# The gate stage of a hybrid decoder block: convolution copies begun by POOL, sums and merges spread over later pieces, sigmoids left in PSUM, gate groups in another order

## The chip, the cores and the metric

The kernel runs on one core of a Trainium2 chip. The metric is the device time of one execution in microseconds. The kernel before was run three times: 1552.89, 1555.58 and 1556.43 us, a median of 1555.58 us. A fourth execution, taken with the profiler, lasted 1552.18 us.

## The reference

One decoder layer over 256 tokens of width 2048, in float32. A normalised input goes through one wide projection `w_in`. Its columns feed two mixers: a chunked gated linear attention with four heads (q, k, v, the decay), and a short gated convolution. Both are merged under sigmoid gates, projected by `w_out`, and followed by a gated feed-forward layer and a last norm. The part that the change touches is this (cut):

```python
def causal_depthwise_conv(u, w):
    s = u.shape[1]
    up = jnp.pad(u, ((0, 0), (CONV_K - 1, 0), (0, 0)))
    return sum(up[:, j:j + s, :] * w[j] for j in range(CONV_K))
...
    y_a = (o * jax.nn.silu(g_out.reshape(b_, s, GLA_HEADS, GLA_HEAD_V))).reshape(b_, s, GLA_VALUE_DIM)
    y_b = gate_b * causal_depthwise_conv(gate_c * xc, conv_w)
    merged = jax.nn.sigmoid(merge_a) * y_a + jax.nn.sigmoid(merge_b) * y_b
    return jnp.einsum('bse,ed->bsd', merged, w_out)
```

## The kernel before

**Pieces.** All weights stream through the core in pieces of 128 x 1024 floats. For each piece SP loads `raw` from DRAM (line 274, or 211 for the sums below), ACT casts it to a rounded part `hi` (line 217), DVE subtracts to get the rest `lo` (line 222), and PE multiplies in three passes, `hi` by the low part of the activations, `lo` by the high part, `hi` by the high part (lines 326 to 328). There are five `raw`, six `hi` and five `lo` buffers. `take` keeps the loading `LOOK = 5` pieces ahead of the piece that PE uses; so the instructions for a later piece stand early in the rows of ACT and DVE, and how far DVE really is ahead of PE at a moment is called its **lead** here.

**Ticks.** Each used piece advances a counter, the tick. `later(n, fn)` and `at(tick, fn)` put other work into the program at a tick, and `one_at_a_time` spaces the PE transposes. In this way work that isn't the stream is woven between the pieces. A scheduler then settles the final row of each engine; every engine works its row in order, and an instruction that waits holds up all behind it.

**Eights and sevens.** In the gate stage, the 520 us in which the columns for the gates g, the convolution (gc, xc, gb) and the merges (ma, mb) are multiplied, there are four blocks of 512 columns for each gate. A single group, an **eight** (for example `ma0`), is eight pieces of 12 matmuls each, and it uses the two PSUM banks `b5` and `ax1`, one for each half of the tokens; so the next eight can begin only when those banks are read out. A pair of groups, a **seven** (`gc0` with `xc0`, and at the end `gb3` with `mb3`), is computed by seven block products in place of eight: 28 pieces of six matmuls. Sixteen of these pieces (called t1 to t4) are sums of weight blocks that DVE makes first (lines 238 and 244), four (called 11) and the last eight (21 and 22) are plain. A seven thus gives DVE much work for little PE time, an eight little work for much PE time, and `mixed` weaves the pieces of eights between those of a seven. The table `GATES` says which eights go with which seven; it has a first entry without a seven and five **steps**. In the steps with two eights, the 16 pieces of eights go between the first 16 entries they may follow, so the last pieces of the seven stand bare.

**Convolution.** When a seven `gc`/`xc` is done, DVE has written the block `u` (lines 411 and 882). `conv_shift` copies `u` into two tiles `u1` and `u2`, shifted by one and two tokens, that is, across partitions: six DMAs begun by ACT (lines 814 to 819), and one more for the taps (line 811). Six ticks later `conv_sum` puts five DVE operations of 128 x 1024 into the program in one go (lines 827 to 831). When the eight `mb` of the block is done, `gated` reads the two PSUM banks through a sigmoid into the single buffer `scr` (ACT, line 847) and multiplies (DVE, line 848), and `merge` adds up (lines 835 and 836) and asks for the transposes (PE line 544, then ACT line 546 and DVE line 547) that the output projection `wo` needs.

**Elsewhere.** `x_blocks` makes the sums of activations for the sevens during the attention stage. The tile `u` has one buffer. The feed-forward stage uses sevens and eights in the same way.

Of the kernel before, what the change touches and what calls it, by code (L numbers as in the profile page):

```python
# [43 lines left out]
def plan():  # L44
# [30 lines left out]
    (("gc0", "xc0"), ("ma0", "gb0")),  # L75
    (("gc1", "xc1"), ("mb0", "g1", "ma1")),
    (("gc2", "xc2"), ("gb1", "mb1", "g2", "ma2")),
# [21 lines left out]
def seven_list(pair):  # L99

    out = [(what, q) for q in range(4) for what in ("11", "t1", "t3", "t2", "t4")]
    return [(pair, e) for e in out + [(what, q) for q in range(4) for what in ("21", "22")]]
# [25 lines left out]
def gates_list():  # L128
    return [e for i, step in enumerate(GATES) for e in mixed(step, i == 4)]
# [36 lines left out]
def block_kernel(ctx, tc, x, xt, cols_in, gkw_in, gku_in, gnw, conv_w, finw, w_in, w_out, w_gu, w_dn, out):  # L166
# [7 lines left out]
    junk_pool = ctx.enter_context(tc.tile_pool(name="junk", bufs=1))  # L174
# [329 lines left out]
    xv = x.rearrange("(t p) d -> p t d", p=P)  # L504

# [9 lines left out]
    def square_sum(src, acc):  # L515
        junk = junk_pool.tile([P, 512], mybir.dt.bfloat16, tag="junk", name="junk")
        nc.scalar.activation(junk[:, :src.shape[-1]], src, AF.Square, accum_out=acc)
# [199 lines left out]
    for q in range(4):  # L717
        at(34 + 6 * q, lambda q=q: x_blocks(q))
# [84 lines left out]
    us, ya, sb = {}, {}, {}  # L803

    def conv_shift(i):
# [8 lines left out]
        nc.scalar.dma_start(u1[1:113, :, :], u[0:112, :, :])  # L814
# [4 lines left out]
        nc.scalar.dma_start(u2[0:2, 1, :], u[126:128, 0, :])  # L819

    def conv_sum(i):
        u, u1, u2, taps = us[i]

        def taps_of(j):
            return taps[:, j:j + 1, :].to_broadcast([P, NT, 512])

        nc.vector.tensor_tensor(out=u2, in0=u2, in1=taps_of(0), op=ALU.mult)
        nc.vector.tensor_tensor(out=u1, in0=u1, in1=taps_of(1), op=ALU.mult)
        nc.vector.tensor_tensor(out=u, in0=u, in1=taps_of(2), op=ALU.mult)
        nc.vector.tensor_tensor(out=u1, in0=u1, in1=u2, op=ALU.add)  # L830
        nc.vector.tensor_tensor(out=u, in0=u, in1=u1, op=ALU.add)

    def merge(i, ts):

        nc.vector.tensor_tensor(out=sb[i][:, ts, :], in0=sb[i][:, ts, :], in1=us[i][0][:, ts, :], op=ALU.mult)
        nc.vector.tensor_tensor(out=sb[i][:, ts, :], in0=sb[i][:, ts, :], in1=ya[i][:, ts, :], op=ALU.add)
# [3 lines left out]
        for t in range(ts.start, ts.stop):  # L840
            one_at_a_time(2, lambda t=t: transpose_block(sb[i][:, t, :], t, mh[i], ml[i]))

    def gated(dst, ps):

        for t in range(NT):
            scr = ew.tile([P, 512], F32, tag="scr", name="scr")
            nc.scalar.activation(scr, ps[t], AF.Sigmoid, scale=r1[:, t:t + 1])
            nc.vector.tensor_tensor(out=dst[:, t, :], in0=dst[:, t, :], in1=scr, op=ALU.mult)

    def gate(key):  # L850
        i = int(key[-1])

        def done(ps):
            if key[:-1] == "g":
                ya[i] = ew.tile([P, NT, 512], F32, tag="ya", name="ya")
# [9 lines left out]
            else:  # L865
                gated(sb[i], ps)
                merge(i, slice(0, NT))
# [3 lines left out]
    def gate_pair(pair):  # L871
# [8 lines left out]
        def done(t, one, two):  # L880
            if pair[0][:-1] == "gc":
                nc.vector.scalar_tensor_tensor(out=two, in0=one, scalar=r1sq[:, t:t + 1], in1=two,
                                               op0=ALU.mult, op1=ALU.mult)
# [33 lines left out]
    h = dpool = None  # L917
# [140 lines left out]

H_AT = (2, 4, 6, 8)
# [56 lines left out]
```

## Time and profile before

| | us |
|---|---|
| three runs, median | 1555.58 |
| profiled execution | 1552.18 |
| its span, first to last instruction | 1550.3 |
| start and attention, 0 to 240 us: PE busy | 232.42 |
| gate stage, 240 to 760 us: PE busy | 494.75 |
| same, DVE busy | 451.87 |
| same, ACT busy | 285.95 |
| output projection, 760 to 840 us: PE busy | 80.00 |
| feed-forward, 840 to 1550 us: PE busy | 701.38 |

A busy PE stands for matmuls that follow one another without a gap. The profile gives, for each instruction that starts after an idle time, the length of that time and the instruction that ended it.

### The profile page before, as it was taken

How to read it: one execution, taken by the hardware profiler on the slowest of the kernel's cores; microseconds unless marked ns; L12 is line 12 of the kernel's file. 1: busy time of each engine (PE TensorE's matmuls, PEld its weight loads, DVE VectorE, ACT ScalarE, POOL GpSimd, SP SyncE). 2: the span in 40 equal slices, each digit the busy share in tenths (PEclk: the TensorE clock that was granted, in tenths of full speed). 3: DMA queues.
4: the chain of work that ended last, by engine and by line, in shares of the span. 5: the costliest groups of instructions: out<-in, count | busy, mean ns of one | idle time of the engine just before them, and what ended most of it. 6: DMA issues, size and time to landing. Idle time of an engine off the chain costs nothing.

```text
span 1550.3 us, 19386 instructions
## 1 busy us (share of the span) xinstructions
PE 1508.5 (97%) x7129; PEld 1256.5 (81%) x7129; DVE 1205.4 (78%) x1208; ACT 839.4 (54%) x947; POOL 20.8 (1%) x33
## 2 busy tenths in 40 slices
PE   9989999989999999889999999999999999999997
PEld 8979988868878787668788888788888888888887
DVE  5887548989879778989768998955889975678664
ACT  6755446645645545456556565633555553455543
POOL 0020000000000000000000000000000000000000
PEclk9999999999999999999999999999999999999999
DMA  9645557877876868768865777866676886676862
GB/s 318 219 149 164 174 162 251 275 237 240 277 229 215 296 176 269 233 209 284 308 181 162 245 229 254 301 206 188 203 262 206 272 281 192 182 222 200 249 222 90
DMA packets 98182, 350.18 MB, mean 226 GB/s; under 512 B 11084, under 2 KB 11212, under 8 KB 97960
## 3 DMA queue, kind: packets, MB, share of 16 engines
q1 hardware_dynamic: 94080, 337.97, 67.3%
q10 hardware_dynamic: 3432, 8.89, 2.3%
q0 software_dynamic: 576, 2.10, 0.4%
q8 instruction: 56, 0.92, 0.2%
q14 instruction: 38, 0.31, 0.1%
HBM read 342.64 MB, written 2.10 MB: 222 GB/s over the span
## 4 chain that ended last, share of the span: by engine, by line
PE 85%; DVE 5%; DMA 4%; issue 2%; ACT 2%; POOL 1%; ACTq 0%; SPq 0%; DVEq 0%
PE fg L326 7%; PE fg L328 7%; PE fg L327 7%; PE dn L326 5%; PE dn L328 5%; PE dn L327 5%; DVE lo L222 3%; PE fu L326 3%; PE fu L327 3%; PE fu L328 3%; PE gc L326 2%; PE gc L328 2%; PE gc L327 2%; DMA raw<-in_w_in_dram 2%; PE ma L326 2%
## 5 line engine op out<-in xcount | busy, mean ns | idle before, releaser
L222 DVE TENSOR_TENSOR lo<-raw,hi 128x1024 fp32r<-128x1024 f32 (+1 forms) x513 | 621.6, 1218 | 194.2 <-PE dn L326 76.3
L217 ACT CAST hi<-raw 128x1024 fp32r<-128x1024 f32 (+1 forms) x513 | 532.8, 1049 | 372.9 <-PE dn L328 116.0
L217 ACT CAST hi<-x 128x1024 fp32r<-128x1024 f32 x120 | 126.3, 1053 | 230.6 <-DVE x L244 153.4
L222 DVE TENSOR_TENSOR lo<-x,hi 128x1024 fp32r<-128x1024 f32 x120 | 146.8, 1223 | 45.4 <-ACT hi L217 32.3
L326 PE MATMUL dn<-lo,acth 128*128 128x512 f32 (+1 forms) x376 | 141.6, 377 | 0.3 <-ACT sg L965 0.3
L327 PE MATMUL dn<-hi,actl 128*128 128x512 f32 (+1 forms) x376 | 141.2, 376 | 0.0
L328 PE MATMUL dn<-hi,acth 128*128 128x512 f32 (+1 forms) x376 | 141.1, 376 | 0.0
L326 PE MATMUL fg<-lo,hh 128*128 128x512 f32 x312 | 122.6, 393 | 0.0
L327 PE MATMUL fg<-hi,hl 128*128 128x512 f32 x312 | 121.6, 390 | 0.0
L328 PE MATMUL fg<-hi,hh 128*128 128x512 f32 x312 | 121.5, 390 | 0.0
L244 DVE TENSOR_TENSOR x<-x,raw 128x1024 f32<-128x1024 f32 x80 | 97.6, 1220 | 4.9 <-DMA raw<-in_w_in_dram 2.6
L326 PEld LDWEIGHTS dn<-lo,acth 128*128 128x128 f32 x376 | 70.8, 188 | 13.4 <-ACT sg L965 0.7
L328 PEld LDWEIGHTS dn<-hi,acth 128*128 128x128 f32 x376 | 70.8, 188 | 12.8
L327 PEld LDWEIGHTS dn<-hi,actl 128*128 128x128 f32 x376 | 70.8, 188 | 12.6
L326 PE MATMUL fu<-lo,hh 128*128 128x512 f32 x192 | 74.7, 389 | 0.0
L328 PE MATMUL fu<-hi,hh 128*128 128x512 f32 x192 | 74.7, 389 | 0.0
L327 PE MATMUL fu<-hi,hl 128*128 128x512 f32 x192 | 74.7, 389 | 0.0
L328 PEld LDWEIGHTS fg<-hi,hh 128*128 128x128 f32 x312 | 58.6, 188 | 12.4
L326 PEld LDWEIGHTS fg<-lo,hh 128*128 128x128 f32 x312 | 58.6, 188 | 12.3 <-ACT hraw L534 0.3
L327 PEld LDWEIGHTS fg<-hi,hl 128*128 128x128 f32 x312 | 58.6, 188 | 11.7
L326 PE MATMUL fg<-lo,sh 128*128 128x512 f32 x160 | 62.9, 393 | 0.0
L328 PE MATMUL fg<-hi,sh 128*128 128x512 f32 x160 | 62.4, 390 | 0.0
(256 smaller groups left out, 3060.6 us busy)
## 6 DMA issues: line engine op xcount, KB each, us to landing
raw<-in_w_in_dram SPq DMA_DIRECT2D x255, 512.0 KB, 4.5
raw<-in_w_gu_dram SPq DMA_DIRECT2D x176, 512.0 KB, 4.5
raw<-in_w_dn_dram SPq DMA_DIRECT2D x88, 512.0 KB, 3.6
raw<-in_w_out_dram SPq DMA_DIRECT2D x32, 512.0 KB, 4.5
y<-in_w_in_dram SPq DMA_DIRECT2D x20, 512.0 KB, 5.3
x<-in_w_in_dram SPq DMA_DIRECT2D x20, 512.0 KB, 4.5
y<-in_w_gu_dram SPq DMA_DIRECT2D x20, 512.0 KB, 5.2
x<-in_w_gu_dram SPq DMA_DIRECT2D x20, 512.0 KB, 6.7
```

The costliest lines, as they stand in the source:

```text
L217: nc.scalar.copy(hi[:, ks, :], raw[:, ks, :])
L222: nc.vector.tensor_tensor(out=lo[:, ks, :], in0=raw[:, ks, :], in1=hi[:, ks, :].bitcast(F32), op=ALU.subtract)
L244: nc.vector.tensor_tensor(out=x, in0=x, in1=other, op=ALU.add)
L326: nc.tensor.matmul(ps, lhsT=sh, rhs=ml, start=first, stop=False, skip_group_check=onto)
L327: nc.tensor.matmul(ps, lhsT=sl, rhs=mh, start=False, stop=False, skip_group_check=onto)
L328: nc.tensor.matmul(ps, lhsT=sh, rhs=mh, start=False, stop=last, skip_group_check=onto)
```

## The change

- The convolution's copies (`conv_shift` and `conv_sum` become one function `conv`) are begun by POOL, one tick after the seven is done in place of two. The shifts of one and of two tokens alternate.
- The five DVE operations of the sum are put in one per tick, `CONV_AT = 12` ticks later and on.
- `merge` waits for the sum (`merge_at`) and at least one tick; its addition comes one tick after its multiplication, its transposes one tick later than before.
- `gated` writes the sigmoid back into the PSUM bank, and DVE multiplies from there. `scr` is gone; `ya` gets two buffers in its place.
- `GATES`: `mb0` moves from step 2 to step 1, `gb1` from step 3 to step 2. Steps 1 to 3 now have three eights each (before two, three and four); steps 4 and 5 keep two.
- In all sevens, the feed-forward's too, the first piece 22 comes one piece later, behind two pieces 21.
- `x_blocks` is asked for at ticks 42 to 57, before 34 to 52. A tile of 128 x 512 that only takes the unused output of squares moves to other pools.

```diff
@@ -72,9 +72,9 @@
 
 GATES = (
     (None, ("g0",)),
-    (("gc0", "xc0"), ("ma0", "gb0")),
-    (("gc1", "xc1"), ("mb0", "g1", "ma1")),
-    (("gc2", "xc2"), ("gb1", "mb1", "g2", "ma2")),
+    (("gc0", "xc0"), ("ma0", "gb0", "mb0")),
+    (("gc1", "xc1"), ("g1", "ma1", "gb1")),
+    (("gc2", "xc2"), ("mb1", "g2", "ma2")),
     (("gc3", "xc3"), ("gb2", "mb2")),
     (("gb3", "mb3"), ("g3", "ma3")),
 )
@@ -99,7 +99,8 @@
 def seven_list(pair):
 
     out = [(what, q) for q in range(4) for what in ("11", "t1", "t3", "t2", "t4")]
-    return [(pair, e) for e in out + [(what, q) for q in range(4) for what in ("21", "22")]]
+    twos = (("21", 0), ("21", 1), ("22", 0), ("21", 2), ("22", 1), ("21", 3), ("22", 2), ("22", 3))
+    return [(pair, e) for e in out + list(twos)]
 
 
 def mixed(step, early=False):
@@ -126,7 +127,7 @@
 
 
 def gates_list():
-    return [e for i, step in enumerate(GATES) for e in mixed(step, i == 4)]
+    return [e for step in GATES for e in mixed(step, step[1][0] == "gb2")]
 
 
 def hidden_list(part):
@@ -513,7 +514,7 @@
 
 
     def square_sum(src, acc):
-        junk = junk_pool.tile([P, 512], mybir.dt.bfloat16, tag="junk", name="junk")
+        junk = (dpool or gpool).tile([P, 512], mybir.dt.bfloat16, tag="junk", name="junk")
         nc.scalar.activation(junk[:, :src.shape[-1]], src, AF.Square, accum_out=acc)
 
     def rstd_of(ss, n, r):
@@ -715,7 +716,7 @@
         sum_blocks(raw, q, xsums, work)
 
     for q in range(4):
-        at(34 + 6 * q, lambda q=q: x_blocks(q))
+        at(42 + 5 * q, lambda q=q: x_blocks(q))
 
 
     def decayed(i, kr, qr):
@@ -800,59 +801,54 @@
     oside = None
     mix = ExitStack()
     mh, ml = [None] * 4, [None] * 4
-    us, ya, sb = {}, {}, {}
-
-    def conv_shift(i):
+    us, ya, sb, merge_at = {}, {}, {}, {}
+
+    def conv(i):
+        u = us[i]
         u1 = ew.tile([P, NT, 512], F32, tag="u1", name="u1")
         u2 = ew.tile([P, NT, 512], F32, tag="u2", name="u2")
         taps = ew.tile([P, 3, 512], F32, tag="taps", name="taps")
-        us[i] = (us[i], u1, u2, taps)
-        u = us[i][0]
-        nc.scalar.dma_start(taps, conv_w[:, :, i * 512:(i + 1) * 512].to_broadcast([P, 3, 512]))
+        nc.gpsimd.dma_start(taps, conv_w[:, :, i * 512:(i + 1) * 512].to_broadcast([P, 3, 512]))
         nc.gpsimd.memset(u1[0:1, 0, :], 0.0)
         nc.gpsimd.memset(u2[0:2, 0, :], 0.0)
-        nc.scalar.dma_start(u1[1:113, :, :], u[0:112, :, :])
-        nc.scalar.dma_start(u1[113:128, :, :], u[112:127, :, :])
-        nc.scalar.dma_start(u1[0:1, 1, :], u[127:128, 0, :])
-        nc.scalar.dma_start(u2[2:114, :, :], u[0:112, :, :])
-        nc.scalar.dma_start(u2[114:128, :, :], u[112:126, :, :])
-        nc.scalar.dma_start(u2[0:2, 1, :], u[126:128, 0, :])
-
-    def conv_sum(i):
-        u, u1, u2, taps = us[i]
+        nc.gpsimd.dma_start(u1[1:113, :, :], u[0:112, :, :])
+        nc.gpsimd.dma_start(u2[2:114, :, :], u[0:112, :, :])
+        nc.gpsimd.dma_start(u1[113:128, :, :], u[112:127, :, :])
+        nc.gpsimd.dma_start(u2[114:128, :, :], u[112:126, :, :])
+        nc.gpsimd.dma_start(u1[0:1, 1, :], u[127:128, 0, :])
+        nc.gpsimd.dma_start(u2[0:2, 1, :], u[126:128, 0, :])
 
         def taps_of(j):
             return taps[:, j:j + 1, :].to_broadcast([P, NT, 512])
 
-        nc.vector.tensor_tensor(out=u2, in0=u2, in1=taps_of(0), op=ALU.mult)
-        nc.vector.tensor_tensor(out=u1, in0=u1, in1=taps_of(1), op=ALU.mult)
-        nc.vector.tensor_tensor(out=u, in0=u, in1=taps_of(2), op=ALU.mult)
-        nc.vector.tensor_tensor(out=u1, in0=u1, in1=u2, op=ALU.add)
-        nc.vector.tensor_tensor(out=u, in0=u, in1=u1, op=ALU.add)
+        for n, (dst, src, by, op) in enumerate(((u1, u1, 1, ALU.mult), (u2, u2, 0, ALU.mult), (u, u, 2, ALU.mult),
+                                                (u1, u1, u2, ALU.add), (u, u, u1, ALU.add))):
+            by = taps_of(by) if isinstance(by, int) else by
+            later(CONV_AT + n, lambda d=dst, s=src, y=by, o=op: nc.vector.tensor_tensor(out=d, in0=s, in1=y, op=o))
 
     def merge(i, ts):
 
-        nc.vector.tensor_tensor(out=sb[i][:, ts, :], in0=sb[i][:, ts, :], in1=us[i][0][:, ts, :], op=ALU.mult)
-        nc.vector.tensor_tensor(out=sb[i][:, ts, :], in0=sb[i][:, ts, :], in1=ya[i][:, ts, :], op=ALU.add)
+        v = sb[i][:, ts, :]
+        nc.vector.tensor_tensor(out=v, in0=v, in1=us[i][:, ts, :], op=ALU.mult)
+        later(1, lambda: nc.vector.tensor_tensor(out=v, in0=v, in1=ya[i][:, ts, :], op=ALU.add))
         if mh[i] is None:
             mh[i] = omain.tile([P, 4, T], F32R, tag=f"m{i}", name="mh")
             ml[i] = oside.tile([P, 4, T], F32R, tag=f"m{i}", name="ml")
         for t in range(ts.start, ts.stop):
-            one_at_a_time(2, lambda t=t: transpose_block(sb[i][:, t, :], t, mh[i], ml[i]))
+            one_at_a_time(3, lambda t=t: transpose_block(sb[i][:, t, :], t, mh[i], ml[i]))
 
     def gated(dst, ps):
 
         for t in range(NT):
-            scr = ew.tile([P, 512], F32, tag="scr", name="scr")
-            nc.scalar.activation(scr, ps[t], AF.Sigmoid, scale=r1[:, t:t + 1])
-            nc.vector.tensor_tensor(out=dst[:, t, :], in0=dst[:, t, :], in1=scr, op=ALU.mult)
+            nc.scalar.activation(ps[t], ps[t], AF.Sigmoid, scale=r1[:, t:t + 1])
+            nc.vector.tensor_tensor(out=dst[:, t, :], in0=dst[:, t, :], in1=ps[t], op=ALU.mult)
 
     def gate(key):
         i = int(key[-1])
 
         def done(ps):
             if key[:-1] == "g":
-                ya[i] = ew.tile([P, NT, 512], F32, tag="ya", name="ya")
+                ya[i] = ew.tile([P, NT, 512], F32, tag=f"ya{i % 2}", name="ya")
                 for t in range(NT):
                     nc.scalar.activation(ya[i][:, t, :], ps[t], AF.Silu, scale=r1[:, t:t + 1])
                 nc.vector.tensor_tensor(out=ya[i], in0=ya[i], in1=o[i], op=ALU.mult)
@@ -864,7 +860,8 @@
                 gated(ya[i], ps)
             else:
                 gated(sb[i], ps)
-                merge(i, slice(0, NT))
+
+                at(max(count["tick"] + 1, merge_at.get(i, 0)), lambda: merge(i, slice(0, NT)))
 
         return done
 
@@ -882,8 +879,8 @@
                 nc.vector.scalar_tensor_tensor(out=two, in0=one, scalar=r1sq[:, t:t + 1], in1=two,
                                                op0=ALU.mult, op1=ALU.mult)
                 if t == 0:
-                    later(2, lambda: conv_shift(i))
-                    later(8, lambda: conv_sum(i))
+                    later(1, lambda: conv(i))
+                    merge_at[i] = count["tick"] + CONV_AT + 7
             else:
                 nc.scalar.activation(two, two, AF.Sigmoid, scale=r1[:, t:t + 1])
                 nc.vector.scalar_tensor_tensor(out=two, in0=one, scalar=r1[:, t:t + 1], in1=two,
@@ -1056,6 +1053,7 @@
     assert not pending and not spaced and not ready and count["loaded"] == len(stream) + 1
 
 
+CONV_AT = 12
 H_AT = (2, 4, 6, 8)
 SQ_AT = (5, 7, 9, 11)
 WARM = 9
```

What this does to the rows of the engines is shown at three places.

**ACT and POOL, the fourth convolution** (`u_5554` and `u_5555` are its tiles u1 and u2). Before, this stood in ACT's row, behind the end of the fourth `gc` seven:

```order
L814 DMA u_5554<-u 112x1024
L815 DMA u_5554<-u 15x1024
L217 CAST hi<-x 128x1024
L217 CAST hi<-raw 128x1024
L816 DMA u_5554<-u 1x16x32
L817 DMA u_5555<-u 112x1024
L818 DMA u_5555<-u 14x1024
L217 CAST hi<-x 128x1024
L819 DMA u_5555<-u 2x512
L217 CAST hi<-raw 128x1024
L217 CAST hi<-x 128x1024
L217 CAST hi<-raw 128x1024
```

Now ACT's row has at that place only casts, and the copies stand in POOL's row, which has nothing else in this stage. For the first convolution (`u_3104` and `u_3105`) it reads:

```order
L811 DMA taps<-in_conv_w_dram 128x3x512
L812 MEMSET u_3104 1x512
L813 MEMSET u_3105 2x512
L814 DMA u_3104<-u 112x1024
L815 DMA u_3105<-u 112x1024
L816 DMA u_3104<-u 15x1024
L817 DMA u_3105<-u 14x1024
L818 DMA u_3104<-u 1x16x32
L819 DMA u_3105<-u 2x512
```

The six DMAs no longer stand between ACT's casts; each cast behind them moves up.

**DVE, the fourth convolution**, from the last write of `u` to the sums, before:

```order
L882 SCALAR_TENSOR_TENSOR u<-gc_0_4848,r1sq,u 128x512
L222 TENSOR_TENSOR lo<-raw,hi 128x1024
L244 TENSOR_TENSOR x<-x,raw 128x1024
L222 TENSOR_TENSOR lo<-x,hi 128x1024
L222 TENSOR_TENSOR lo<-raw,hi 128x1024
L244 TENSOR_TENSOR x<-x,y 128x1024
L828 TENSOR_TENSOR u_5554<-u_5554,taps 128x1024
L222 TENSOR_TENSOR lo<-x,hi 128x1024
L238 TENSOR_TENSOR raw<-y,x 128x1024
L244 TENSOR_TENSOR x<-x,raw 128x1024
L222 TENSOR_TENSOR lo<-raw,hi 128x1024
L827 TENSOR_TENSOR u_5555<-u_5555,taps 128x1024
```

and now, up to the first of the five operations (`u_5521` is u1; all five now carry line 827):

```order
L879 SCALAR_TENSOR_TENSOR u<-gc_0_4835,r1sq,u 128x512
L222 TENSOR_TENSOR lo<-raw,hi 128x1024
L244 TENSOR_TENSOR x<-x,raw 128x1024
L222 TENSOR_TENSOR lo<-x,hi 128x1024
L222 TENSOR_TENSOR lo<-raw,hi 128x1024
L244 TENSOR_TENSOR x<-x,y 128x1024
L222 TENSOR_TENSOR lo<-x,hi 128x1024
L222 TENSOR_TENSOR lo<-raw,hi 128x1024
L244 TENSOR_TENSOR x<-x,raw 128x1024
L238 TENSOR_TENSOR raw<-y,x 128x1024
L827 TENSOR_TENSOR u_5521<-u_5521,taps 128x1024
L222 TENSOR_TENSOR lo<-x,hi 128x1024
```

The first operation on the copies now has nine other DVE operations between it and the last write of `u` in place of five, and the other four follow at rows further down with two to six operations between most of them.

**DVE, the end of the eight `ma0`**, before (`scr` is the sigmoid's output in SBUF):

```order
L244 TENSOR_TENSOR x<-x,y 128x1024
L222 TENSOR_TENSOR lo<-raw,hi 128x1024
L848 TENSOR_TENSOR ya<-ya,scr 128x512
L222 TENSOR_TENSOR lo<-x,hi 128x1024
L848 TENSOR_TENSOR ya<-ya,scr 128x512
L244 TENSOR_TENSOR x<-x,raw 128x1024
L222 TENSOR_TENSOR lo<-raw,hi 128x1024
```

and now, with the PSUM banks `ma_0` and `ma_1` as operands:

```order
L244 TENSOR_TENSOR x<-x,y 128x1024
L222 TENSOR_TENSOR lo<-raw,hi 128x1024
L844 TENSOR_TENSOR ya<-ya,ma_0_2343 128x512
L844 TENSOR_TENSOR ya<-ya,ma_1_2344 128x512
L222 TENSOR_TENSOR lo<-x,hi 128x1024
L222 TENSOR_TENSOR lo<-raw,hi 128x1024
L244 TENSOR_TENSOR x<-x,raw 128x1024
```

The two multiplications now stand next to each other. In the rows of PE, ACT and DVE of the attention stage nothing has moved.

More of the change, by code (lines that the diff above doesn't have):

```diff
@@ L173, in block_kernel @@
     wlo = ctx.enter_context(tc.tile_pool(name="wlo", bufs=5))
-    junk_pool = ctx.enter_context(tc.tile_pool(name="junk", bufs=1))
     aT = ctx.enter_context(tc.tile_pool(name="aT", bufs=1))
@@ L504, in block_kernel @@
     xv = x.rearrange("(t p) d -> p t d", p=P)
+    dpool = None
     xs0 = wraw.tile([P, 4, T], F32, tag="raw", name="xs")
@@ L916, in block_kernel @@
     ssh = const.tile([P, NT, 4], F32, name="ssh")
-    h = dpool = None
+    h = None
     for n in range(4):
```

## Prediction

> **What bounds the kernel now.** I read the page first, the busy time of the engines.
>
> ```profile
> PE 1508.5 (97%) x7129; PEld 1256.5 (81%) x7129; DVE 1205.4 (78%) x1208; ACT 839.4 (54%) x947; POOL 20.8 (1%) x33
> ```
>
> PE is busy for 97% of the span, so the most that any change to waits can bring is about 42 us. Where those lie is read from the busy time in windows, one for each stage.
>
> ```profile
> 240.00:760.00 520.00, 494.75 (x2163) 402.25 (x2162) 451.87 (x419) 285.95 (x300) 4.56 (x8) 0.99 0.76 246
> 760.00:840.00 80.00, 80.00 (x370) 66.38 (x369) 55.08 (x58) 45.87 (x62) 1.56 (x3) 1.00 0.63 199
> 840.00:1535.00 695.00, 694.28 (x3143) 575.48 (x3142) 535.40 (x507) 366.01 (x393) 0.00 (x0) 1.00 0.70 224
> ```
>
> The first number behind the window is its length, then come PE's and PEld's busy us, DVE's, ACT's and POOL's. The feed-forward stage loses 0.72 us until its last 15 us, the output projection nothing. The gate stage loses 520 - 494.75 = 25.25 us, with DVE busy for 87% of it. That is what this change works on. The timeline of PE in the stage shows each stop: start, length, engine, line, and in brackets the idle time before it and who ended it.
>
> ```profile
> 276.79 0.50 PE L326 MATMUL gb<-lo,xh 128*128 128x512 f32 x1 [0.63 <-ACT scr L847]
> 335.77 0.79 PE L326 MATMUL mb<-lo,xh 128*128 128x512 f32 x1 [5.65 <-DVE lo L222]
> 441.82 0.50 PE L326 MATMUL gb<-lo,xh 128*128 128x512 f32 x1 [1.11 <-DVE lo L222]
> 529.14 0.50 PE L326 MATMUL ma<-lo,xh 128*128 128x512 f32 x1 [1.56 <-ACT ya L857]
> 570.95 0.50 PE L326 MATMUL gb<-lo,xh 128*128 128x512 f32 x1 [0.71 <-DVE lo L222]
> 584.57 0.50 PE L326 MATMUL gb<-lo,xh 128*128 128x512 f32 x1 [1.05 <-DVE lo L222]
> 639.29 0.50 PE L326 MATMUL gc<-lo,xh 128*128 128x512 f32 x1 [1.27 <-DVE lo L222]
> 643.82 0.66 PE L544 MATMUL trb<-ident,sb 128*128 128x128 f32 x4 [2.43 <-DVE ml L547]
> 661.36 0.50 PE L326 MATMUL gb<-lo,sh 128*128 128x512 f32 x1 [1.73 <-DVE lo L222]
> 667.92 0.50 PE L326 MATMUL gb<-lo,sh 128*128 128x512 f32 x1 [2.15 <-DVE lo L222]
> 671.43 0.50 PE L326 MATMUL g<-lo,xh 128*128 128x512 f32 x1 [1.86 <-DVE lo L222]
> 682.78 0.50 PE L326 MATMUL g<-lo,xh 128*128 128x512 f32 x1 [1.54 <-DVE lo L222]
> 757.19 0.63 PE L544 MATMUL trb<-ident,sb 128*128 128x128 f32 x4 [1.21 <-DVE sb L836]
> ```
>
> These are 22.9 us; the rest of the 25.25, 2.35 us, is six stops of 0.2 to 0.55 us between 589 and 745 us. Nearly all name DVE's `lo`, which is late because something ahead of it in a row was. The first convolution shows what, in the timelines of ACT and DVE ("ACTq" is ACT's sequencer, which begins the copies; the two rows of 654 and 665 us are the fourth convolution):
>
> ```profile
> 322.20 0.63 ACTq L814 DMA_DIRECT2D u<-u  x1
> 326.37 1.30 ACTq L819 DMA_DIRECT2D u<-u  x1
> 327.77 1.05 ACT L217 CAST hi<-raw 128x1024 fp32r<-128x1024 f32 x1 [5.10 <-DVE raw L238]
> ...
> 330.63 1.23 DVE L828 TENSOR_TENSOR u<-u,taps 128x1024 f32<-128x1024 f32 x1 [3.77 <-DMA u<-u]
> ...
> 654.68 0.74 DVE L882 SCALAR_TENSOR_TENSOR u<-gc,r1sq,u 128x512 f32<-128x512 f32 x1
> ...
> 665.50 1.23 DVE L828 TENSOR_TENSOR u<-u,taps 128x1024 f32<-128x1024 f32 x1 [1.93 <-DMA u<-u]
> ```
>
> From 322.20 to 327.67 ACT does nothing but begin six copies, and casts nothing. Then DVE stops for 3.77 us at the first operation on the copies, with the subtractions that PE needs behind it in its row. PE runs out of pieces at 330 and stands for 5.65 us. So the stage isn't short of an engine; it is short of DVE's lead at the four convolutions, and in steps 4 and 5, which have little slack to win it back.
>
> **The change part by part.** *PE's time for a piece:* from the window 240 to 320 us below, 79.37 us for 350 matmuls, 0.227 us each; a piece of a seven (six) is 1.36 us, of an eight (twelve) 2.72 us. *DVE's:* the starts of two operations that follow without a gap are 1.14 us apart for 1024 columns and 0.60 for 512.
>
> ```profile
> 240.00:320.00 80.00, 79.37 (x350) 65.13 (x349) 75.67 (x70) 51.48 (x53) 0.00 (x0) 1.00 0.78 258
> ...
> 339.61 0.39 PE L326 MATMUL mb<-lo,xh 128*128 128x512 f32 x1
> ...
> 574.22 1.21 DVE L827 TENSOR_TENSOR u<-u,taps 128x1024 f32<-128x1024 f32 x1
> 575.36 1.22 DVE L829 TENSOR_TENSOR u<-u,taps 128x1024 f32<-128x1024 f32 x1
> ...
> 640.29 0.68 DVE L398 TENSOR_TENSOR v<-gc,v 128x512 f32<-128x512 f32 x1
> 640.89 1.21 DVE L222 TENSOR_TENSOR lo<-raw,hi 128x1024 fp32r<-128x1024 f32 x1
> ```
>
> *Copies begun by POOL, first convolution:* the 5.65 us go. So does what follows them: nine matmuls from 335.77 to 339.61 take 3.84 us where nine at 0.227 take 2.04, so 1.8 us more. The Trainium skill, page "TensorE: Matmul & The Clock Gate", part 1, says why: after about 3.4 us without work the gate halves TensorE's clock; the trace agrees, since only the stop of 5.65 us is followed by such matmuls.
>
> *Copies and sums, the other three:* 1.11 (second) and 0.71 (third) are stops right behind ACT's copies. 1.05 and, of the small stops, 1.65 lie in step 4 behind the third's five sums in one go; 1.73, 2.15, 1.86 and 1.54 behind the fourth's copies and sums, and 0.2 just ahead. Together 12.0 us.
>
> What is late next? DVE's work in step 4 against PE's. The bare end (four sums, eight plain pieces, the first of step 5) is 13 x 1.36 + 1.1 for the transposes = 18.8 us of PE. DVE has 4 x 2.28 + 9 x 1.14 = 19.4 for pieces, about 4.3 for the seven's combinations, 1.2 and 2.3 for gate and merge, 1.2 for `ml`: 28.4 us. The 9.6 us missing are covered if DVE comes with a full lead, four sum pieces, 9.1 us. Before, it waited for the third convolution's copies at the start of the step; now it can come with a full lead, since steps 1 to 3 each have three eights: 68 operations for the pieces, 77.5 us, 4.3 for the combinations, 9.2 for sums, merge and `ml`, 3.5 for the gates, 94.5 us of DVE against 28 x 1.36 + 24 x 2.72 = 103.4 of PE. But step 5 begins with the lead spent, its fourth sum of 5.7 us comes in its second quarter, and a quarter wins only 2.9 us (five pieces of 1.36 and four of 2.72 on PE, 13 operations of 1.14 on DVE). In the new row DVE also has two `x` sums there with `lo<-x` directly behind; the row below prices that wait for ACT at 34.4 / 37 = 0.9 us. I leave 3.0 us of stops in steps 4 and 5: bounds 0 (lead full) and 9.6 (no lead).
>
> ```profile
> DVE lo L222 <- ACT hi L217: 34.4, 37, 2.7
> DVE u L828 <- DMA u<-u: 15.3, 4, 5.0
> ...
> L926 POOL DMA_DIRECT2D h<-in_x_dram x4: 724/727/857, 758.5 to 760.8; - x4
> ...
> DMA to landing us min/median/max: 6.7/8.1/10.9
> ...
> DMA to landing us min/median/max: 4.5/6.2/7.4
> ```
>
> *Will POOL's copies be in time?* POOL begins the load of `h` four times at 0.73 us each, and these land after 6.7 to 10.9 us; the copies begun by ACT landed after 4.5 to 7.4 (last row). Six from POOL take 6 x 0.73 = 4.4 us to begin, so `u1` is there between 3.6 + 4.5 = 8 and 4.4 + 10.9 = 15 us after `u`; by ACT it was 655.4 to 665.5, 10.1 us. DVE has nine operations between, 9 x 1.14 = 10.3, plus two waits for ACT: 12 us when it is catching up, and some 26 (13 ticks at about 2 us) when PE sets the pace. A wait is thus 0 to 3 us, in two of the four convolutions; I take 0.5 in all. The 15.3 us that DVE waited go otherwise. POOL itself is idle, nothing stands behind the copies but the next ones and, after the stage, `h`.
>
> The Trainium skill, page "SBUF — State Buffer", in its box on the DVE that blocks a DMA, speaks against this move: descriptors for a POOL DMA can't be written while DVE runs an operation in a two-port mode. It gives copies and `tensor_scalar` such modes, `tensor_tensor` none. By that rule the sum stays as it is here, since DVE's row in the stage is two-operand work only, and the four `h` loads agree: 0.73 us each beside the `lo` subtractions.
>
> *Merges in two ticks and later:* 1.27, 2.43 and 1.21 us are stops in which transposes or pieces wait behind the merge. The order on DVE in the bare end is almost the old one, only one more piece (1.36 us) stands between the transposes; half goes, 2.4 us, bounds 0 and 4.9.
>
> *Sigmoids in PSUM:* the counts stay. An operand in PSUM costs DVE nothing (0.682 against 0.684 us below); a sigmoid written to PSUM isn't in the trace, it takes ACT 0.69 now, and I keep that. At half or double the time, the five places named below would win 1.7 or pay 3.4 us.
>
> ```profile
> L848 DVE TENSOR_TENSOR ya<-ya,scr 128x512 f32<-128x512 f32 x8 | 5.5, 684 | 0.0
> L398 DVE TENSOR_TENSOR v<-gc,v 128x512 f32<-128x512 f32 x4 | 2.7, 682 | 0.0
> ...
> L847 ACT ACTIVATE scr<-ma,r 128x512 f32<-128x512 f32 x8 | 5.5, 688 | 3.0 <-DVE ya L848 2.9
> ```
>
> New is a wait: the first bank is free after DVE's multiplication, not after ACT's sigmoid, 0.69 us later, and the next eight's first matmul stands in PE's row behind it. The second bank comes no later, since its sigmoid no longer waits for `scr`. One or two bare pieces (1.4 to 2.7 us) lie between at five places (`ma0`, `mb0`, `ma1`, `mb1`, `ma2`). I take +1.0, bounds 0 and 5 x 0.69 = 3.4. The stops of 0.63 and 1.56 are of this kind and stay.
>
> *At nothing:* the twos' order (PE waits for no `pb` for more than 0.2 us; the feed-forward loses 0.72 us in all), `x_blocks` (no row moves), the scratch tile. Their cover is PE's own row; without it each would cost at most those 0.7 us. Some eleven restarts fall away, 0.11 us each (0.50 for a first matmul against 0.39): -1.2.
>
> The sum: -5.65 - 1.8 - 12.0 - 2.4 - 1.2 + 3.0 + 0.5 + 1.0 = -18.6 us, on the profiled 1552.2: 1533.6. The three timed runs lay 0.7, 3.4 and 4.3 us above that execution, so I put 1.4 on top: **1535**.
>
> **The rivals.** *DVE stays the limit of steps 4 and 5.* For it speaks that DVE is busy 52.12 of 58 us from 602 to 660; against it that it had just waited for copies (15.3 us in four convolutions) and for the casts behind them. Then only 5.65, 1.8, 1.11 and 0.71 go, 0.5 of restarts, and 1.0 is added: -8.8 and 1543.4, with the 1.4 about **1545**.
>
> ```profile
> 602.00:660.00 58.00, 53.22 (x231) 42.13 (x230) 52.12 (x51) 30.49 (x35) 0.00 (x0) 1.00 0.77 244
> ```
>
> *Banks held by DVE's row.* The multiplication stands behind the subtractions for four pieces ahead. If DVE comes to those five places with a lead of one piece, PE waits for three sum pieces less what it has between: 3 x 2.28 - 2.7 = 4.1 us. Five of them, 20 us, eat the gain: 1554 on the median. Against it: the sigmoid stood equally far back in ACT's row before, and only 0.63 us came of it.
>
> *Slower: POOL's copies land too late.* DVE then stands at the first sum of each convolution, as it did for 5.0 us at most. PE feels it once the landing exceeds DVE's 12 us plus a lead of 8, 20 us; the gain of 18.6 is gone at 4.6 us more each. At a landing after 30 us it is 4 x 10 = 40 us lost, **1574**. Against it: `h`'s 10.9 us at most, of four times the same queue. For it: seven requests with up to 768 KB in the same queue have not been seen.
>
> **How the numbers follow.** My forecast 0.64, with 1526 to 1541; DVE's limit 0.18; held banks 0.07; late copies 0.11. The range begins where every stop is gone, 1552.2 - 25.25 - 1.8 - 2.0 + 1.4 = 1524.5, so **1524**, and ends above DVE's limit with the 5 us that its bounds give, **1550**; held banks and late copies stay out. Within 0.2% (3.1 us) of 1555.58 is about what measuring can't tell from no change. Faster is the first two, 0.82; same is held banks, 0.07; slower is late copies, 0.11.
>
> **What would show it.** After: no row of ACT's sequencer with `u`; no DVE wait for the copies over 3 us; no PE stop over 3 us in the gate stage, all granted clock there 1.00; PE idle there 6 to 9 us, most of it in steps 4 and 5 and at the transposes. PE waiting for a sigmoid's multiplication by more than 1 us at the five places shows the held banks. If the first sum waits over 5 us for a copy, POOL is the step that failed. A longer `lo` or cast, or raw pieces landing later, would be a cost that I have not counted.

## The result and the profile after

| | before | after |
|---|---|---|
| median of four runs, us | 1554.53 (1552.89 to 1556.43) | 1537.06 (1536.11 to 1538.17) |
| ratio, 95% interval | | 0.9888 (0.9870 to 0.9905) |
| profiled execution, its span, us | 1552.18, 1550.3 | 1536.89, 1535.2 |
| first transpose behind the gate stage, us | 757.19 | 743.92 |

The kernel became faster by 17.5 us on the medians and by 15.3 us on the two profiled executions. The page's busy times of the engines, and its DMA queues, after the change:

```profile
PE 1507.4 (98%) x7129; PEld 1256.3 (82%) x7129; DVE 1206.8 (79%) x1208; ACT 840.4 (55%) x947; POOL 36.7 (2%) x61
...
q0 software_dynamic: 2944, 9.41, 2.5%
q10 hardware_dynamic: 432, 1.57, 0.3%
```

The busy times of PE, DVE and ACT differ by at most 1.4 us from those before; POOL has 16 us more, the copies that it now begins (q0). The windows of the gate stage, the output projection and the feed-forward stage:

```profile
240.00:745.00 505.00, 490.57 (x2152) 398.81 (x2151) 451.71 (x417) 285.76 (x299) 18.09 (x33) 1.00 0.77 252
745.00:825.00 80.00, 80.00 (x366) 66.25 (x365) 54.11 (x58) 45.34 (x62) 2.95 (x4) 1.00 0.63 200
825.00:1535.00 710.00, 702.52 (x3211) 583.95 (x3210) 541.75 (x520) 371.94 (x404) 0.00 (x0) 1.00 0.70 223
```

PE now stands for 14.43 us in the gate stage, before for 25.25, and the granted clock there is 1.00 where it was 0.99. The stops in PE's timeline, all but the one of 0.20 us:

```profile
241.58 0.50 PE L326 MATMUL gc<-lo,sh 128*128 128x512 f32 x1 [0.30 <-ACT ya L853]
378.77 0.50 PE L326 MATMUL ma<-lo,xh 128*128 128x512 f32 x1 [0.49 <-ACT ya L853]
416.84 0.50 PE L326 MATMUL gb<-lo,xh 128*128 128x512 f32 x1 [1.00 <-DVE ya L844]
486.93 0.50 PE L326 MATMUL g<-lo,xh 128*128 128x512 f32 x1 [1.75 <-DVE sb L844]
492.29 0.63 PE L545 MATMUL trb<-ident,sb 128*128 128x128 f32 x4 [0.53 <-DVE sb L833]
526.17 0.50 PE L326 MATMUL ma<-lo,xh 128*128 128x512 f32 x1 [1.24 <-ACT ya L853]
591.63 0.50 PE L326 MATMUL mb<-lo,xh 128*128 128x512 f32 x1 [1.19 <-ACT sb L858]
632.85 0.50 PE L326 MATMUL gc<-lo,xh 128*128 128x512 f32 x1 [1.01 <-DVE lo L222]
639.45 0.50 PE L326 MATMUL gc<-lo,xh 128*128 128x512 f32 x1 [1.67 <-DVE lo L222]
643.99 0.50 PE L326 MATMUL gb<-lo,xh 128*128 128x512 f32 x1 [0.16 <-DVE lo L222]
651.10 0.50 PE L326 MATMUL gb<-lo,sh 128*128 128x512 f32 x1 [0.56 <-DVE lo L222]
655.79 0.50 PE L326 MATMUL gb<-lo,sh 128*128 128x512 f32 x1 [0.29 <-DVE lo L222]
661.47 0.50 PE L326 MATMUL gb<-lo,xh 128*128 128x512 f32 x1 [1.30 <-DVE lo L222]
680.77 0.50 PE L326 MATMUL gb<-lo,xh 128*128 128x512 f32 x1 [1.27 <-DVE lo L222]
743.92 0.63 PE L545 MATMUL trb<-ident,sb 128*128 128x128 f32 x4 [1.01 <-DVE sb L833]
```

Together with that one they come to 13.97 us. Three kinds are left: lines 844, 853 and 858, an eight that waits for its PSUM banks (5.97 us); `lo`, pieces late in steps 4 and 5 (6.26 us from 632 us on); `trb`, the merges' transposes (1.54 us). The first convolution, in the timelines of POOL and DVE:

```profile
341.21 0.61 POOL L814 DMA_DIRECT2D u<-u  x1 [118.22 <-DVE u L879]
343.88 0.52 POOL L819 DMA_DIRECT2D u<-u  x1
...
352.94 1.23 DVE L244 TENSOR_TENSOR x<-x,raw 128x1024 f32<-128x1024 f32 x1 [0.47 <-DMA raw<-in_w_in_dram]
354.08 1.22 DVE L222 TENSOR_TENSOR lo<-raw,hi 128x1024 fp32r<-128x1024 f32 x1
355.22 1.22 DVE L827 TENSOR_TENSOR u<-u,taps 128x1024 f32<-128x1024 f32 x1
```

POOL begins six copies in 3.2 us, and DVE comes to the first sum 14.0 us after the first was begun, without a wait.

### The profile page after: what moved, and what is told of

Same layout as the page of the kernel before. It is cut to its first block, busy times and chain, and to the rows that moved or that the text cites. A ratio compares the mean times of both kernels' runs of the same rounds, so it can differ in the third digit from the quotient of the medians.

```text
span 1535.2 us, 19387 instructions
## 1 busy us (share of the span) xinstructions
PE 1507.4 (98%) x7129; PEld 1256.3 (82%) x7129; DVE 1206.8 (79%) x1208; ACT 840.4 (55%) x947; POOL 36.7 (2%) x61
## 4 chain that ended last, share of the span: by engine, by line
PE 82%; DVE 9%; issue 4%; ACT 2%; DMA 2%; POOL 1%; DVEq 0%; SPq 0%; ACTq 0%
PE fg L326 7%; PE fg L328 7%; PE fg L327 7%; PE dn L326 5%; PE dn L327 5%; PE dn L328 5%; DVE lo L222 4%; PE fu L326 3%; PE fu L327 3%; PE fu L328 3%; PE gc L326 2%; PE gc L328 2%; PE gc L327 2%; DVE x L244 2%; PE wo L328 2%
```

## The experiments

The table has each run's ratio to the kernel before, timed beside it on the same chip (its medians there were 1554.5, 1554.8 and 1553.5), and from the profile the sum of PE's stops from 230 to 790 us. The last two columns come from DVE's row: how many operations stand between the last write of `u` and the first sum, for the four convolutions, and how long DVE waited for the copies in all.

| run | median us | ratio (interval) | PE's stops | operations | DVE waits |
|---|---|---|---|---|---|
| before | | 1 | 25.05 | 4, 4, 4, 5 | 15.3 |
| after_again | 1537.70 | 0.9895 (0.9874 to 0.9917) | 13.53 | 13, 10, 11, 9 | 0 |
| pool_only | 1540.23 | 0.9914 (0.9897 to 0.9931) | 14.08 | 9, 7, 8, 5 | 2.4 |
| act_copies | 1556.35 | 1.0015 (1.0006 to 1.0024) | 25.86 | 16, 5, 4, 5 | 8.2 |
| act_extra | 1567.55 | 1.0090 (1.0071 to 1.0109) | 34.55 | 6, 5, 3, 5 | 24.2 |
| pool_extra | 1544.55 | 0.9940 (0.9924 to 0.9956) | 17.27 | 13, 10, 11, 9 | 0 |
| at4 | 1537.86 | 0.9893 (0.9871 to 0.9914) | 11.68 | 9, 8, 9, 8 | 0.9 |
| psum_only | 1549.28 | 0.9959 (0.9943 to 0.9974) | 19.95 | 4, 4, 4, 5 | 13.8 |
| pool_psum | 1539.26 | 0.9907 (0.9885 to 0.9928) | 14.63 | 9, 7, 6, 5 | 5.7 |
| sums_once | 1534.06 | 0.9868 (0.9853 to 0.9883) | 9.13 | 13, 10, 11, 9 | 0 |
| old_order | 1534.27 | 0.9872 (0.9858 to 0.9887) | 11.14 | 11, 11, 11, 9 | 0 |
| order_sums | 1533.90 | 0.9866 (0.9845 to 0.9887) | 13.78 | 11, 11, 11, 9 | 0 |
| better | 1526.37 | 0.9817 (0.9797 to 0.9837) | 4.59 | 11, 13, 8, 12 | 0 |

### Who begins the copies

**act_copies**, the changed kernel with all seven DMAs of `conv` begun by ACT again (one of the seven lines):

```diff
-        nc.gpsimd.dma_start(u1[1:113, :, :], u[0:112, :, :])
+        nc.scalar.dma_start(u1[1:113, :, :], u[0:112, :, :])
```

> The changed kernel with one thing undone: the convolution's seven DMAs are begun by ACT again, at the new ticks. Theory (ACT's row blocked by beginning the copies is most of what went): ACT is held for about 5.4 us at each of four convolutions while DVE's lead of some 8 us covers a part, so 4 to 9 us come back, about 1541 to 1546 us, with ACT's casts waiting 3 to 5 us behind the copies and PE stops of 1 us and more at the four places; DVE no longer waits for the copies, since the sums stand 13 ticks behind. Rival (who begins the copies is incidental, the later and spread sums made the gain): within 1.5 us of the changed kernel's 1537.1.

Measured: 1556.35 us. Not a part but the whole gain went, 19.3 us. The first convolution in the timelines of ACT (ACTq is its sequencer), DVE and PE:

```profile
341.33 0.64 ACTq L814 DMA_DIRECT2D u<-u  x1
346.77 0.67 ACTq L819 DMA_DIRECT2D u<-u  x1
347.54 1.05 ACT L217 CAST hi<-raw 128x1024 fp32r<-128x1024 f32 x1 [5.28 <-PE gc L328]
...
352.39 1.22 DVE L244 TENSOR_TENSOR x<-x,raw 128x1024 f32<-128x1024 f32 x1 [5.21 <-DMA raw<-in_w_in_dram]
...
354.80 0.50 PE L326 MATMUL g<-lo,xh 128*128 128x512 f32 x1 [3.34 <-DVE lo L222]
```

ACT is held for 6.1 us and starts no cast. The first sum stands 16 operations behind `u` here, so DVE waits for no copy; it waits 5.21 us for a raw piece, and PE stops for 3.34 us all the same. That piece isn't late: it is there at 352.4 us, in the changed kernel at 352.9. But there five subtractions stand ahead of the operation that needs it, and here they stand behind it. The third convolution, in the timelines of ACT and DVE:

```profile
575.43 0.66 ACT L843 ACTIVATE ma<-ma,r 128x512 f32<-128x512 f32 x1 [5.34 <-DMA u<-u]
...
576.13 0.69 DVE L844 TENSOR_TENSOR ya<-ya,ma 128x512 f32<-128x512 f32 x1 [3.81 <-ACT ma L843]
580.88 1.23 DVE L827 TENSOR_TENSOR u<-u,taps 128x1024 f32<-128x1024 f32 x1 [4.07 <-DMA u<-u]
```

DVE waits 3.81 us for a sigmoid that ACT can begin only behind its six copies, and then 4.07 us for the copies themselves. At the third and fourth convolutions the sum stands 4 and 5 operations behind `u` although it was asked for 12 ticks later, and DVE waits 4.1 us for copies at each. So ACT's part does harm in two ways: it holds casts and sigmoids, and the rows that the scheduler makes for such a kernel have waiting operations ahead of the subtractions. That the rows change with the engine that begins the copies is shown; that the scheduler does so because it reckons with late casts is my reading.

**pool_only**, the kernel before with only the engine of the seven DMAs changed (the order of the copies, the ticks and the rest as before; one of the seven lines):

```diff
-        nc.scalar.dma_start(u1[1:113, :, :], u[0:112, :, :])
+        nc.gpsimd.dma_start(u1[1:113, :, :], u[0:112, :, :])
```

> The kernel before with one thing changed: the convolution's seven DMAs are begun by POOL; the sums stay six ticks behind the copies and in one go. Theory (two waits, ACT's for beginning and DVE's for the landing): ACT's 5 us go, but the copies land 8 to 11 us after u, so DVE still stops at the first sum for 2 to 6 us; the gain is 3 to 8 us on the kernel before, about 1547 to 1551 us. Rival 1 (ACT's row was all): 12 us and more, 1542 us or less. Rival 2 (copies from POOL land much later): DVE stops for over 8 us each and the time is 1554 us or more.

Measured: 1540.23 us, 14.3 us faster than before on the same chip. The first rival was right: this edit alone brings most of the 17.5 us, with the sums still asked for six ticks behind and in one go. In its rows the first sum stands 5 to 9 operations behind `u`, before 4 or 5.

**act_extra** and **pool_extra**, the changed kernel with six more transfers of the same sizes from `u` to unused places in DRAM, begun by ACT or by POOL:

```diff
+        more = nc.dram_tensor(f"more_{i}", (2, P, NT, 512), F32, kind="Internal").ap()
+        for a, b, c in ((0, 0, 112), (1, 0, 112), (0, 112, 127), (1, 112, 126)):
+            nc.scalar.dma_start(more[a, b:c, :, :], u[b:c, :, :])
+        nc.scalar.dma_start(more[0, 127:128, 0, :], u[127:128, 0, :])
+        nc.scalar.dma_start(more[1, 126:128, 0, :], u[126:128, 0, :])
```

> The changed kernel, whose copies POOL still begins, with the same six transfers begun once more by ACT at the place where ACT began the copies before; they go to an unused place in DRAM and nobody waits for them. Theory (ACT's row is held while it begins them, and the casts behind it come late): 10 to 19 us slower than the changed kernel, 1547 to 1556, with PE stops of 3 to 5 us behind lo at the convolutions, whose casts wait behind the six. Rival (DVE waiting for the landing of the copies was the cost, and beginning them costs ACT nothing that PE feels): 1537 to 1540.

> The same as the run before, but POOL begins the second six transfers too. The control for the traffic: theory (what the extra transfers cost comes from ACT's row and not from the DMA engines): within 3 us of the changed kernel, 1535 to 1541. Rival (transfers of some 1 MB at each convolution make the pieces' loads late, whoever begins them): as slow as the run with ACT.

Measured: 1567.55 us by ACT, 1544.55 us by POOL. Both lie above the ranges that I had given. The traffic costs some 7 us: DVE's waits for the loads of the sums' blocks in the control, after_again,

```profile
DVE raw L238 <- DMA y<-in_w_in_dram: 4.7, 3, 1.8
```

and in pool_extra:

```profile
DVE raw L238 <- DMA y<-in_w_in_dram: 8.4, 4, 3.7
```

The same transfers begun by ACT cost another 23.0 us. The first convolution with ACT, in the timelines of ACT, DVE and PE:

```profile
338.59 4.14 ACTq L822 DMA_DIRECT2D more<-u  x4
344.03 1.87 ACTq L824 DMA_DIRECT2D more<-u  x1
345.99 1.05 ACT L217 CAST hi<-raw 128x1024 fp32r<-128x1024 f32 x1 [6.48 <-issue]
...
352.16 1.23 DVE L832 TENSOR_TENSOR u<-u,taps 128x1024 f32<-128x1024 f32 x1 [7.73 <-DMA u<-u]
...
354.58 0.79 PE L326 MATMUL g<-lo,xh 128*128 128x512 f32 x1 [5.85 <-DVE lo L222]
```

ACT is held for 7.3 us though nobody needs these transfers. POOL's copies are begun from 338.86 us on, but the first sum now stands six operations behind `u` in place of 13, comes too early and waits 7.73 us, with the subtractions for five casts of 346 to 351 us behind it. The copies that it waits for are also later: with ACT's transfers begun at the same moment they land after 7.7, 11.0 and 12.4 us (least, median, most), in the changed kernel after 4.9, 7.9 and 9.5; in pool_extra, where the extra transfers stand behind them in POOL's row, they land after 9.0 at most. So pool_extra is not a full control for the traffic. The theory has the direction and a size too small, and the 23 us have three parts: ACT's row held, the row that the scheduler makes of it, and copies that land some 3 us later. How they divide can't be told from these runs.

### How late the copies may be needed

**at4**, the changed kernel with the sums asked for earlier:

```diff
-CONV_AT = 12
+CONV_AT = 4
```

> The changed kernel with the first sum 4 ticks behind the copies in place of 12. Theory (the copies land 4.9 to 9.5 us after POOL begins them, and DVE has 4 ticks of 1.36 to 2.7 us until it needs them, less its lead of some 8 us): DVE waits 4 to 8 us for u1 at each convolution, PE stops of 1 to 4 us behind lo follow, 1542 to 1550. Rival (the lead and the spread sums swallow the wait, as for the kernel before with POOL alone and 6 ticks): 1536 to 1539, DVE's waits for copies under 8 us in all.

Measured: 1537.86 us, the same as the control's 1537.70 on another chip (ratios 0.9893 and 0.9895). The rival was right: DVE waited 0.9 us once. Four ticks still leave 8 or 9 operations between `u` and the first sum. Where only five stand there, at the fourth convolution of pool_only, DVE waits 1.35 us, and at that of **pool_psum** (below) more; DVE's and PE's timelines:

```profile
656.24 1.23 DVE L828 TENSOR_TENSOR u<-u,taps 128x1024 f32<-128x1024 f32 x1 [3.60 <-DMA u<-u]
...
658.65 0.80 PE L326 MATMUL gb<-lo,sh 128*128 128x512 f32 x1 [3.82 <-DVE lo L222]
```

### The other edits

**psum_only**, the kernel before with the sigmoid left in its bank:

```diff
-            scr = ew.tile([P, 512], F32, tag="scr", name="scr")
-            nc.scalar.activation(scr, ps[t], AF.Sigmoid, scale=r1[:, t:t + 1])
-            nc.vector.tensor_tensor(out=dst[:, t, :], in0=dst[:, t, :], in1=scr, op=ALU.mult)
+            nc.scalar.activation(ps[t], ps[t], AF.Sigmoid, scale=r1[:, t:t + 1])
+            nc.vector.tensor_tensor(out=dst[:, t, :], in0=dst[:, t, :], in1=ps[t], op=ALU.mult)
```

> The kernel before with the sigmoid written back to its PSUM bank and nothing else; scr is gone, the copies are still begun by ACT. Theory by the prediction's term (banks held until DVE's multiplication, +1.0, bounds 0 to 3.4; the gated eights' own stops grew by 2.8 us in the changed kernel): 1 to 3 us slower than before, the stops named by L846 or L847 ahead of gb1 and g2. Rival (the held banks of the changed kernel come from its order of the gate groups, which puts ma1 and gb1 next to each other with no bare piece between): within 0.7 us of before.

Measured: 1549.28 us, 5.5 us faster, which neither foresaw. No eight waits longer for its banks than before: the stop of 0.63 us is gone, and 1.56 became 1.39. So the held banks of the changed kernel go with its order of the eights, as the rival had it. What the 5.5 us come from I can only argue: ACT no longer waits for `scr` (2.9 us before, three times, with casts behind), and PE's stops of 1.11 and 0.71 us, and 2.43 at the transposes, are gone (one of 1.87 us behind the seven's combinations is new at that place).

**pool_psum**, the kernel before with the edits of pool_only and psum_only together:

> The kernel before with two edits: the copies begun by POOL, and the sigmoid left in its PSUM bank. Theory (these two are the whole gain and add up, 14.3 and 5.5 us alone; order, spread sums, later merges and x_blocks bring nothing or cost 2 us): 1534 to 1536.5, ratio to before 0.987, not slower than the changed kernel. Rival (the four other edits bring some 3 us, and the two overlap because both remove stops behind the same rows of ACT): 1538 to 1541.

Measured: 1539.26 us. The two do not add up: 14.3 and 5.5 us alone, 14.2 together. PE's stops say the same: 11.0 and 5.1 us fewer alone, 10.4 together. The changed kernel's control, timed on another chip, has a ratio lower by 0.0012, which is 1.9 us and inside the intervals; so what the other edits bring together can't be told from nothing.

**after_again, sums_once, old_order, order_sums**: the changed kernel once more, and with the five sums at one tick, with the old table, and with both.

```diff
-            later(CONV_AT + n, lambda d=dst, s=src, y=by, o=op: nc.vector.tensor_tensor(out=d, in0=s, in1=y, op=o))
+            later(CONV_AT, lambda d=dst, s=src, y=by, o=op: nc.vector.tensor_tensor(out=d, in0=s, in1=y, op=o))
```

```diff
-    (("gc0", "xc0"), ("ma0", "gb0", "mb0")),
-    (("gc1", "xc1"), ("g1", "ma1", "gb1")),
-    (("gc2", "xc2"), ("mb1", "g2", "ma2")),
+    (("gc0", "xc0"), ("ma0", "gb0")),
+    (("gc1", "xc1"), ("mb0", "g1", "ma1")),
+    (("gc2", "xc2"), ("gb1", "mb1", "g2", "ma2")),
```

> The changed kernel with the five DVE operations of a convolution's sum put in at one tick, 12 ticks after the copies, in place of one per tick. Theory: 5 x 1.14 = 5.7 us in one go fit into DVE's lead of 8 us in steps 2 to 4 and cost 1 to 2 us in step 5, so 1537 to 1539 us. Rival (spreading is what made the gain): every sum breaks the lead, 3 us and more at each of four, 1546 us or more.

> The changed kernel with the old table of gate groups (two, three, four, two and two eights in the five steps). Theory: steps 4 and 5 are unchanged and step 3 has four eights' worth of slack either way, so the order alone is worth 0 to 3 us, 1537 to 1540 us. Rival (balance of DVE's work between the steps made the gain): 6 us and more come back, 1543 us or more, as new PE stops in steps 1 and 2.

> The changed kernel itself, as the control beside the next three. Theory (the new order of the gate groups and the sums one per operand each cost about 3 us): it lies at 1536 to 1538, about 17.5 us under before, and 3 us over the versions with the old order and with the sums in one go, which gave 1534.3 and 1534.1. Rival (those two edits change nothing, and the 3 us are a difference between occasions): it lies at 1534 to 1535, ratio to before 0.987.

> The changed kernel with both the old order of the gate groups and the five sums at one tick. Theory (each edit costs about 3 us, by its own stops): both go, 1531 to 1533, ratio to before 0.985. Rival (neither matters): as the control, within 1 us. Second rival (the edits stand in for each other, so that undoing both brings the old stops behind the sums back): 1537 to 1541, with stops of 1 to 2 us in step 4 behind the third convolution's five operations, as in the kernel before.

Measured: 1534.06, 1534.27 and 1533.90 us without the edits, 1537.06 and 1537.70 with both. Undoing either or both gives some 3 us, so they don't add up, and none of the three lies in a range that I had given. No run shows a gain from either edit; that they cost 3 us is likely but not settled, since the intervals with and without them overlap.

**better**, the changed kernel with three eights (`mb0`, `gb1`, `ma2`) one step later, so that steps 2 to 4 have three each, and with the product of the sigmoid and the convolution taken early, which frees `u` (cut):

```diff
-    (("gc0", "xc0"), ("ma0", "gb0", "mb0")),
-    (("gc1", "xc1"), ("g1", "ma1", "gb1")),
-    (("gc2", "xc2"), ("mb1", "g2", "ma2")),
-    (("gc3", "xc3"), ("gb2", "mb2")),
+    (("gc0", "xc0"), ("ma0", "gb0")),
+    (("gc1", "xc1"), ("mb0", "g1", "ma1")),
+    (("gc2", "xc2"), ("gb1", "mb1", "g2")),
+    (("gc3", "xc3"), ("gb2", "ma2", "mb2")),
...
+    def times_u(i):
+        nc.vector.tensor_tensor(out=sb[i], in0=sb[i], in1=us[i], op=ALU.mult)
...
+                if i in (1, 2):
+                    at(max(count["tick"] + 1, merge_at[i]), lambda: times_u(i))
```

> The changed kernel with the eights in other steps (two in step 1, three in steps 2, 3 and 4, two in step 5) and the product of the second and third convolutions with the sigmoid taken ahead of the merge. Theory (steps 4 and 5 are short of DVE's lead by some 6 us, since a seven asks 94.5 us of DVE for 103.4 of PE with three eights, and more than PE takes with two): the stops behind lo from 630 us on fall from 6.3 us to 1 to 3, in all 1531 to 1534. Rival (DVE's work in the whole stage is what is short, so a stop taken from step 4 comes back in another step): the sum of PE's stops in the stage stays at 12 to 15 us, 1535 to 1538.

Measured: 1526.37 us, 11.3 us under the control beside it, 4.6 us below the range of the theory, and the fastest of all. All stops of PE in its gate stage from 500 us on:

```profile
566.23 0.50 PE L326 MATMUL ma<-lo,xh 128*128 128x512 f32 x1 [1.65 <-ACT sb L862]
635.28 0.63 PE L545 MATMUL trb<-ident,sb 128*128 128x128 f32 x4 [0.34 <-DVE sb L837]
732.26 0.63 PE L545 MATMUL trb<-ident,sb 128*128 128x128 f32 x4 [1.09 <-DVE sb L837]
```

From there on no piece comes late. The last 60 us of step 4, of the changed kernel:

```profile
585.00:645.00 60.00, 55.96 (x247) 45.05 (x246) 53.98 (x52) 33.34 (x36) 0.52 (x1) 1.00 0.72 233
```

and of this one:

```profile
580.00:640.00 60.00, 59.66 (x267) 48.96 (x266) 50.22 (x49) 35.55 (x38) 0.00 (x0) 1.00 0.75 237
```

PE gets 3.7 us more done while DVE works 50.22 us in place of 53.98: the third eight brings PE work that needs less of DVE. The table and the early product were not run apart.

## Why the prediction was right or wrong

The time was forecast at 1535 us and came to 1537.06. By its steps, in the profiled execution:

| step | forecast | measured |
|---|---|---|
| first convolution's stop and the slow matmuls behind it | gone, -7.45 | gone |
| other stops behind copies and sums | -12.0, then +3.0 left in steps 4 and 5 | 5.25 left |
| merges, 4.91 before | 2.45 left | 2.55 left (1.01 + 0.53 + 1.01) |
| DVE waiting for POOL's copies | 0.5 | 0 |
| eights waiting for banks, 2.19 before | 3.2 left | 5.97 left |
| gate stage's PE idle | 6 to 9 | 14.43 |

(The 1.01 at 632.85 us is at the place of the 1.27 that the merges were charged with; the stop of 0.20 us belongs to none.) With these sizes and the 0.20 the forecast's -18.6 becomes -13.8; the first transpose behind the stage came 13.3 us earlier. The other 1.8 us of the span lie behind that transpose, which in the 14 profiles takes 791.3 to 793.1 us, with the old order of the pieces 21 and 22 as with the new: this is variation, and nothing is to be seen of that edit, which was costed at nothing. That the medians differ by 17.5 us is in part luck of the sample: the profiled run of before was faster than all four timed ones. It is luck, too, that the time was missed by 2.1 us where the terms were missed by 4.8: the 1.8 us behind the transpose, and the 1.4 us put on top for the timed runs, fell the right way. And the 6 to 9 us of idle time don't follow from the prediction's own terms, which leave 9.7 of the 25.25.

*Right:* POOL's copies are the heart of it, in size (19.45 us forecast for the stops behind copies and sums, 14.3 and 19.3 measured from both sides), and they are in time: the rival of late copies fell, in at4 too. No stop is over 1.75 us, and no row of ACT's sequencer has `u`.

The Trainium skill, page "DMA: Bandwidth & Descriptors", section "Issuing engine by pattern", gives simple loads and stores to Sync and calls the queues of sync and scalar generally faster. The landing of the copies points the same way, though the trace has it for only five of ACT's 24 copies: 4.5, 6.2 and 7.4 us (least, median, most) by ACT before; 5.2, 6.8 and 8.7 by POOL in pool_only, with the copies in the same order; and by POOL after

```profile
DMA to landing us min/median/max: 4.9/7.9/9.5
```

In pool_only the kernel is still 14.3 us faster with copies that land later, so the later landing weighs less here than ACT's row.

*Right in size, incomplete in mechanism:* the prediction had ACT's casts held and DVE waiting for copies, and reckoned the distance from `u` to the sum in the ticks asked for. The runs show the distance to depend on who begins the copies: 4 or 5 operations at three convolutions with ACT at 12 ticks, 8 or 9 with POOL at 4. It also put 2.7 us of stops in step 4 (1.05 and 1.65) down to five sums in one go; sums_once and pool_only ask for them in one go too, and no piece comes late at that place.

*Wrong, the steps that failed:* "Sigmoids in PSUM ... I take +1.0". The banks held by DVE's multiplication cost 2.75 us (1.00 at `gb1`, 1.75 at `g2`; of this kind were 0.63 before), inside the bounds; but alone this edit gained 5.5 us. I had counted the bank that comes free later and left out the buffer that no longer holds ACT. The other eights' waits, for ACT to read the banks of `g` and `gb`, were forecast to stay at 1.56 and came to 3.22 us. And "I leave 3.0 us of stops in steps 4 and 5": 5.25 us were left. The reason given, a step 5 that begins with the lead spent, fits what better shows: with a third eight in step 4 no stop behind `lo` is left there.

## What to carry to other kernels

An instruction that begins a DMA stands in its engine's row like any other. On ACT, whose row feeds the critical one here, six of them took 4 to 7 us of that row at a time, and the scheduler then put other work ahead of its data; put them on an idle engine first, before distances are tuned. Then look at the order in which the work is woven: work that is dear for the feeding engine needs work beside it that is cheap for it, in every step.

Gains of single edits need not add up: 14.3 and 5.5 gave 14.2. An edit is judged on top of the others, not by itself.

## What the runs showed of the hardware

*Beginning a DMA.* ACT took 0.56 to 2.11 us for each copy in act_copies' first convolution, 6.1 us for six; POOL took 0.51 to 0.61 for each of the 24 after, 3.2 us for six, with DVE at two-operand work beside it. (Of the four `h` loads that the prediction leaned on, only the last two ran beside a `lo` subtraction.)

*The clock after short stops.* The prediction tied slow matmuls to a stop over 3.4 us. They came after shorter ones too, though not after all. In pool_extra, PE's timeline:

```profile
490.28 0.79 PE L326 MATMUL g<-lo,xh 128*128 128x512 f32 x1 [2.11 <-DVE sb L849]
490.87 0.63 PE L327 MATMUL g<-hi,xl 128*128 128x512 f32 x1
...
493.43 0.50 PE L327 MATMUL g<-hi,xl 128*128 128x512 f32 x1
493.77 0.39 PE L328 MATMUL g<-hi,xh 128*128 128x512 f32 x1
```

For 3.5 us the matmuls start 0.43 us apart in place of 0.23, some 1.6 us lost behind a stop of 2.11 us; the granted clock in these 3.5 us was 0.52. In order_sums a stop of 2.04 us, and in pool_psum one of 2.30 us, was followed by matmuls at full pace and a granted clock of 1.00:

```profile
341.56 0.50 PE L326 MATMUL mb<-lo,xh 128*128 128x512 f32 x1 [2.30 <-DVE lo L222]
341.89 0.40 PE L327 MATMUL mb<-hi,xl 128*128 128x512 f32 x1
```

*Sigmoids.* Written to PSUM they took ACT 0.658 us (median of eight, after), written to SBUF 0.690. The Trainium skill, page "ScalarE: Activation LUTs", section "Step-by-step: what each stage is for", says that ScalarE reaches PSUM faster than SBUF; the trace agrees, by 0.03 us.
